# The second MLP product as seven quarter products (Strassen), with sums made by accumulating DMA

## The chip, the cores and the metric

The kernel runs on one core of a Trainium2 chip. The time is that of one execution on the device, in microseconds (us). The engines are TensorE (PE; its weight loads are shown as PEld), VectorE (DVE), ScalarE (ACT), GpSimd (POOL) and SyncE (SP), which only issues transfers.

## What is computed

One layer of a decoder trunk: four token mixers, gated and projected, then a two-layer MLP. The change touches the MLP alone. S = 512 tokens, D = 1024, hidden width 4096, all in 32-bit floats.

```python
hn = _rms(x, norm2_g[l])
hid = jnp.square(jax.nn.relu(jnp.einsum('bsd,df->bsf', hn, w_mlp1[l])))
x = x + jnp.einsum('bsf,fd->bsd', hid, w_mlp2[l])
```

## The kernel before

Every product with weights is made of three matmuls: each operand is split into a high part (`hi`, a cast by ScalarE, L74) and a low part (`lo`, the difference, a subtraction by VectorE, L75), and `mm3` (L78 to L81) adds high x high, high x low and low x high in PSUM. The first factor of a matmul stays in the array (128 x 128), the second streams through it, at most 512 columns.

Weights come as a stream of pieces of 512 KB (`piece`, L91). A piece has a `load` (a transfer on SyncE's queue into one of 4 buffers `raw`, L102) and a `make` (the split into `hi_m` and `lo_m`, 3 buffers each). `take` and `get` (L114 to L126) make two pieces ahead of the one in use and load two more. A buffer of `raw` comes free when its `lo` is made; one of `hi_m` when its matmuls are done. The order on each engine is settled by the framework's planner from its own estimate of readiness, within these dependencies.

The MLP begins at L946. The first product computes the hidden values transposed, 128 hidden rows by 512 tokens at a time (a piece `m1`: 8 x 3 = 24 matmuls into the PSUM tile `h`); `mlp1_done` (L958) applies relu on ScalarE, squares on VectorE and splits the result into `hdh` and `hdl`. This is done for half of the hidden rows (16 pieces), then the second product of this half follows (L986 to L1019): for each half `q` of the 1024 columns, 8 pieces `m2` of 256 hidden rows by 512 columns, each with 4 token tiles x 2 x 3 = 24 matmuls into four PSUM tiles `o`. After the last piece VectorE adds each `o` to `X1` (the residual, L1017), and in the second half SyncE stores the result (L1019). The last token tile's last columns are made as two halves of 256. Then the same for the second half of the hidden rows.

GpSimd issues some transfers in the attention part, among them copies from SBUF to SBUF (L402, L403); none in the MLP.

Of the kernel before, what the change touches and what calls it, by code (L numbers as in the profile page):

```python
# [8 lines left out]
F32 = mybir.dt.float32  # L9
# [7 lines left out]
P = 128  # L17
# [10 lines left out]
HPW = 268  # L28

# [8 lines left out]
def block_kernel(ctx: ExitStack, tc: tile.TileContext, x, w_in, w_branch, w_gate, w_out,  # L38
# [52 lines left out]
    def piece(name, srcs, nk, alloc=None):  # L91
# [22 lines left out]
    def get(i, ahead):  # L114
        while len(made) < min(i + 1 + ahead, len(pieces)):
            made.append(pieces[len(made)][1]())
        for j in range(len(made), min(len(made) + 2, len(pieces))):
            pieces[j][0]()
        return made[i]
# [40 lines left out]
    for q in range(2):  # L160
        for k in range(4):
            piece(f"wo{q}{k}", [w_out[k * 256 : (k + 1) * 256, q * 512 : (q + 1) * 512]], 2,
                  lambda tag, nm: wop[0].tile([P, 4 * HPW], F32R, tag=tag, name=f"{tag}_{nm}"))
    NH = NF // 2
    for fh in range(2):
        for f in range(fh * NH, (fh + 1) * NH):
            piece(f"m1_{f}", [w_mlp1[:, f * P : (f + 1) * P]], 8)
        for q in range(2):
            for f0 in range(fh * NH, (fh + 1) * NH, 2):
                piece(f"m2_{q}{f0}", [w_mlp2[f0 * P : f0 * P + 256, q * 512 : (q + 1) * 512]], 2)  # L170

# [795 lines left out]
    for fh in range(2):
        f = fh * NH
        if fh == 0:
            finish(*ttr[:2])  # L970
            w = take(3, 0)
            accs = [ps(f"h_{f + j}") for j in range(3)]
            for j in range(3):
                mlp1_part(accs[j], w[j], 0, 256)
            finish(*ttr)
            for j in range(3):
                mlp1_part(accs[j], w[j], 256, 512)
                mlp1_done(f + j, accs[j])
            f += 3
        while f < (fh + 1) * NH:  # L980
            w, = take()
            acc = ps(f"h_{f}")
            mlp1_part(acc, w, 0, 512)
            mlp1_done(f, acc)
            f += 1
        for q in range(2):  # L986
            if q == 0:
                acc = [ps(f"o_{fh}{q}{t}") for t in range(NT)]
            else:
                a2 = [ps2(f"o_{fh}{q}{t}") for t in range(2)]  # L990
                acc = [a2[t // 2][:, t % 2, :] for t in range(NT)]
            acc = [[(a, 0, 512)] for a in acc]
            if fh == 1 and q == 1:
                acc[-1] = [(ps(f"o_{fh}{q}h{i}")[:, :256], 256 * i, 256) for i in range(2)]

            def out_mm(fp, t, w, part):
                sl = slice(t * P, (t + 1) * P)
                a, c0, n = part
                for j in range(2):
                    h = hid[fh * NH + 2 * fp + j]  # L1000
                    mm3(a, (h[0][:, sl], h[1][:, sl]), (w[0][:, j, c0 : c0 + n], w[1][:, j, c0 : c0 + n]),
                        fp == 0 and j == 0, fp == NH // 2 - 1 and j == 1)


            for fp in range(NH // 2 - 2):
                w, = take()
                for t in range(NT):
                    for part in acc[t]:
                        out_mm(fp, t, w, part)
            w = take(2, 1)  # L1010
            for t in range(NT):
                for part in acc[t]:
                    for i in range(2):
                        out_mm(NH // 2 - 2 + i, t, w[i], part)
                    a, c0, n = part
                    cs = slice(q * 512 + c0, q * 512 + c0 + n)
                    nc.vector.tensor_tensor(out=X1[:, t, cs], in0=X1[:, t, cs], in1=a, op=ALU.add)  # L1017
                    if fh == 1:
                        nc.sync.dma_start(out[t * P : (t + 1) * P, cs], X1[:, t, cs])  # L1019
# [49 lines left out]
```

## Time and profile before

| | |
|---|---|
| median of 3 runs | 832.59 us (832.59 to 832.61) |
| profiled execution: from the first to the last instruction (span) | 831.0 us |
| profiled execution with what lies around the span (taken as the median) | 832.6 us |
| TensorE busy | 822.4 us, 4097 matmuls |
| VectorE busy | 426.7 us |
| ScalarE busy | 299.6 us |
| transfers | 81.34 MB, mean 98 GB/s |

Busy time is the time in which at least one instruction of the engine was under way. The record of a matmul is longer than its share of the engine, since the next one enters before it ends: the distance of two starts is what one costs.

### The profile page before, as it was taken

The page shows a single profiled execution, that of the slowest core. Times are in us where ns is not written, and L with a number is a line of the kernel's source. Part 1 is how long each engine was busy: PE and PEld are TensorE (multiplying, and loading weights), DVE is VectorE, ACT ScalarE, POOL GpSimd, SP SyncE. Part 2 cuts the span into 40 slices and gives each one's busy share as a digit, 9 for nine tenths or more (in the row PEclk, how much of TensorE's full clock was granted, in tenths as well). Part 3 has the DMA queues.
Part 4 walks back from the last instruction along what each step waited for, and adds up shares of the span by engine and source line. Part 5 has one row for each costly group of instructions (what it writes and reads, how often), then busy time and mean ns, then how long its engine had stood idle before and what let it go on. Part 6 is the DMA issues. An engine that isn't in the chain of part 4 may idle for free.

```text
span 831.0 us, 10391 instructions
## 1 busy us (share of the span) xinstructions
PE 822.4 (99%) x4097; PEld 674.7 (81%) x4097; DVE 426.7 (51%) x766; ACT 299.6 (36%) x507; POOL 86.1 (10%) x82
## 2 busy tenths in 40 slices
PE   7999999999999999999999999999999999999998
PEld 5989787777787888888888888888888888888887
DVE  5967764346999446734625754442232444442321
ACT  6636533444423325423515344341121334332110
POOL 6011011221443121220000000000000000000000
PEclk9999999999999999999999999999999999999999
DMA  9282222321222232333536032323233233223401
GB/s 307 81 196 60 87 66 79 87 77 52 63 65 89 77 91 87 97 93 91 198 142 175 3 102 80 98 103 101 77 102 102 81 96 102 101 77 102 152 26 51
DMA packets 108979, 81.34 MB, mean 98 GB/s; under 512 B 3873, under 2 KB 96321, under 8 KB 108930
## 3 DMA queue, kind: packets, MB, share of 16 engines
q1 hardware_dynamic: 107666, 76.61, 30.4%
q10 hardware_dynamic: 720, 2.62, 0.9%
q0 software_dynamic: 544, 1.45, 0.6%
q8 instruction: 32, 0.52, 0.3%
q14 instruction: 17, 0.14, 0.0%
HBM read 78.05 MB, written 2.10 MB: 96 GB/s over the span
## 4 chain that ended last, share of the span: by engine, by line
PE 97%; DMA 1%; SPq 1%; ACT 0%; DVE 0%; issue 0%
PE gt L79 7%; PE gt L81 7%; PE h L81 7%; PE h L79 7%; PE h L80 7%; PE gt L80 7%; PE o L79 7%; PE o L80 7%; PE o L81 7%; PE pj L79 2%; PE pj L81 2%; PE wo L80 2%; PE wo L79 2%; PE wo L81 2%; PE pj L80 2%; PE pv L548 2%
## 5 line engine op out<-in xcount | busy, mean ns | idle before, releaser
L75 DVE TENSOR_TENSOR lo_m<-raw_m,hi_m 128x1024 fp32r<-128x1024 f32 x64 | 78.4, 1225 | 176.8 <-ACT hi_m L74 176.8
L74 ACT CAST hi_m<-raw_m 128x1024 fp32r<-128x1024 f32 x64 | 67.1, 1049 | 195.9 <-PE o L81 107.1
L81 PE MATMUL h<-HH,lo_m 128*128 128x512 f32 (+1 forms) x280 | 104.9, 375 | 0.0
L79 PE MATMUL h<-HH,hi_m 128*128 128x512 f32 (+1 forms) x280 | 104.5, 376 | 0.2 <-ACT HH L74 0.2
L80 PE MATMUL h<-HL,hi_m 128*128 128x512 f32 (+1 forms) x280 | 104.5, 374 | 0.0
L79 PE MATMUL gt<-XH,hi_wg 128*128 128x512 f32 x256 | 101.8, 398 | 0.0
L81 PE MATMUL gt<-XH,lo_wg 128*128 128x512 f32 x256 | 101.2, 395 | 0.0
L80 PE MATMUL gt<-XL,hi_wg 128*128 128x512 f32 x256 | 100.7, 393 | 0.0
L79 PE MATMUL o<-hi_m,hdh 128*128 128x512 f32 x240 | 95.0, 396 | 0.0
L80 PE MATMUL o<-lo_m,hdh 128*128 128x512 f32 x240 | 94.9, 395 | 0.0
L81 PE MATMUL o<-hi_m,hdl 128*128 128x512 f32 x240 | 94.3, 394 | 0.0
L75 DVE TENSOR_TENSOR lo_wg<-raw_wg,hi_wg 128x1024 fp32r<-128x1024 f32 x32 | 39.1, 1222 | 61.9 <-ACT hi_wg L74 61.8
L74 ACT CAST hi_wg<-raw_wg 128x1024 fp32r<-128x1024 f32 x32 | 33.5, 1047 | 83.0 <-PE gt L80 57.9
L81 PEld LDWEIGHTS h<-HH,lo_m 128*128 128x128 f32 x280 | 52.7, 188 | 10.4
L80 PEld LDWEIGHTS h<-HL,hi_m 128*128 128x128 f32 x280 | 52.7, 188 | 10.2
L79 PEld LDWEIGHTS h<-HH,hi_m 128*128 128x128 f32 x280 | 52.3, 188 | 10.1 <-ACT HH L74 0.5
L526 POOL TENSOR_SCALAR p<-p,c 128x128 f32<-128x128 f32 (+3 forms) x32 | 42.8, 1347 | 153.8 <-DVE c L524 141.8
L81 PEld LDWEIGHTS gt<-XH,lo_wg 128*128 128x128 f32 x256 | 48.1, 188 | 11.8 <-issue 0.5
L80 PEld LDWEIGHTS gt<-XL,hi_wg 128*128 128x128 f32 x256 | 48.2, 188 | 10.7
L79 PEld LDWEIGHTS gt<-XH,hi_wg 128*128 128x128 f32 x256 | 48.1, 188 | 10.7 <-issue 0.3
L81 PEld LDWEIGHTS o<-hi_m,hdl 128*128 128x128 f32 x240 | 45.0, 188 | 11.0
L79 PEld LDWEIGHTS o<-hi_m,hdh 128*128 128x128 f32 x240 | 45.2, 188 | 10.6
(368 smaller groups left out, 1439.8 us busy)
## 6 DMA issues: line engine op xcount, KB each, us to landing
raw_m<-in_w_mlp_dram SPq DMA_DIRECT2D x64, 512.0 KB, 3.6
raw_wg<-in_w_gate_dram SPq DMA_DIRECT2D x32, 512.0 KB, 3.9
raw_wb<-in_w_branch_dram SPq DMA_DIRECT2D x16, 256.0 KB, 2.6
raw_wo<-in_w_out_dram SPq DMA_DIRECT2D x8, 512.0 KB, 4.2
x<-in_x_dram SPq DMA_DIRECT2D x4, 512.0 KB, 6.6
raw_kv<-in_w_in_dram SPq DMA_DIRECT2D x4, 512.0 KB, 4.7
w<-in_cmp_w_dram SPq DMA_DIRECT2D x4, 512.0 KB, 6.0
X<-in_x_dram ACTq DMA_DIRECT2D x4, 512.0 KB, 6.7
```

Source lines behind the costliest of these rows:

```text
L74: i = nc.scalar.copy(hi, src)
L75: (eng or nc.vector).tensor_tensor(out=lo, in0=src, in1=f32(hi), op=ALU.subtract)
L79: nc.tensor.matmul(dst, l[0], r[0], start=start, stop=False)
L80: nc.tensor.matmul(dst, l[0], r[1], start=False, stop=False)
L81: nc.tensor.matmul(dst, l[1], r[0], start=False, stop=stop)
L526: nc.gpsimd.tensor_scalar_mul(p_[:, b, :w], p_[:, b, :w], c2[:, b : b + 1])
L548: nc.tensor.matmul(dst[i], V[:, k, b, g * HD : (g + 1) * HD], pts[h - 1 + i][:, b, k * P : (k + 1) * P], start=False, stop=b == 1 and k == t)
```

## The change

The second product is hidden (512 x 4096) times weights (4096 x 1024). Both are cut in two by two quarters: hidden by token half `h` and half `k` of the hidden rows, weights by `k` and column half `n`. Seven products of quarters (256 x 2048 by 2048 x 512) replace the eight; each takes a quarter or a sum or difference of two from either side, and is added to or subtracted from one or two quarters of `X1`. `PROD` lists for each product the left quarters (h, k, sign), the right quarters (k, n, sign) and the targets (h, n, sign).

A quarter product goes in 8 pieces of 256 hidden rows: a weight piece of 256 x 512 and a left piece of 2 x 128 rows by 256 tokens, with 2 x 2 x 3 = 12 matmuls of 512 columns. The hidden values stay unsplit in one tile `HID`; the left piece is split when it is needed (tags `hc0`, `hc1`). Sums of weights (products 3, 4, 6, 7): the first quarter's piece is loaded by SyncE into one of 3 buffers `rsum`, and an accumulating DMA that GpSimd issues adds the second quarter's to it. A difference of weights (product 1): both are loaded and VectorE subtracts. Sums of left pieces (1, 6, 7): SyncE copies the first inside SBUF to one of 4 buffers `hc`, and an accumulating DMA adds the second. Differences of left pieces (2, 5): VectorE.

The order is: the first 16 pieces of the first product; then the other 16, each followed by a piece of product 3 (8 times) or 6 (8 times); then products 4, 2, 1, 5, 7. Products 1 to 6 gather in a PSUM tile of two banks and are added to `X1` by operations of 128 x 1024; finished quarters are stored after products 2, 1 and 5. Product 7 ends as the old kernel did, with a 512-wide tile and two of 256. The constants `RAWS` and `AHEAD` have the old values 4 and 2.

```diff
@@ weight stream @@
+    PROD = {
+        1: (((0, 0, 1), (1, 1, 1)), ((0, 0, 1), (1, 1, -1)), ((0, 0, 1), (1, 1, -1))),
+        2: (((1, 1, 1), (1, 0, -1)), ((0, 0, 1),), ((1, 0, -1), (1, 1, 1))),
+        3: (((0, 0, 1),), ((0, 1, 1), (1, 1, 1)), ((0, 1, 1), (1, 1, -1))),
+        4: (((1, 1, 1),), ((1, 0, 1), (0, 0, 1)), ((0, 0, -1), (1, 0, 1))),
+        5: (((0, 0, 1), (0, 1, -1)), ((1, 1, 1),), ((0, 0, 1), (0, 1, -1))),
+        6: (((1, 0, 1), (0, 0, 1)), ((0, 0, 1), (0, 1, 1)), ((1, 1, 1),)),
+        7: (((0, 1, 1), (1, 1, 1)), ((1, 0, 1), (1, 1, 1)), ((0, 0, 1),)),
+    }
+    hcp = []
+    def block_piece(name, prod, p, B, kh, A):
+        aq, bq, _ = PROD[prod]
+        st = {}
+        def load():
+            if st:
+                return
+            st["raw"] = raws = []
+            for i, (k, n, sign) in enumerate(bq):
+                r0 = (k * kh + 2 * p) * P
+                wv = B[r0 : r0 + 256, n * 512 : (n + 1) * 512].rearrange("(k p) c -> p k c", p=P)
+                if i and sign > 0:
+                    nc.gpsimd.dma_start(raws[0].rearrange("p (k c) -> p k c", k=2), wv, accum_op=ALU.add)
+                    continue
+                if len(bq) == 1 or i:
+                    raw = wp.tile([P, 4 * HPW], F32, tag="raw", name=f"raw_{name}{i}", bufs=RAWS)[:, :1024]
+                else:
+                    raw = hcp[0].tile([P, 1024], F32, tag="rsum", name=f"rsum_{name}", bufs=3)
+                nc.sync.dma_start(raw.rearrange("p (k c) -> p k c", k=2), wv)
+                raws.append(raw)
+            st["a"] = src = [A()[:, k * kh + 2 * p : k * kh + 2 * p + 2, h * 256 : (h + 1) * 256] for h, k, _ in aq]
+            if len(aq) == 2:
+                hs = hcp[0].tile([P, 2, 256], F32, tag="hc", name=f"hc_{name}", bufs=4)
+                if aq[1][2] > 0:
+                    nc.sync.dma_start(hs, src[0])
+                    nc.gpsimd.dma_start(hs, src[1], accum_op=ALU.add)
+                    del src[1]
+                src.append(hs)
+        def make():
+            load()
+            raw = st["raw"]
+            if len(raw) == 2:
+                nc.vector.tensor_tensor(out=raw[0], in0=raw[0], in1=raw[1], op=ALU.subtract)
+            w = [walloc(tag, name)[:, :1024] for tag in ("hi", "lo")]
+            split(raw[0], w[0], w[1])
+            src = st["a"]
+            if len(src) == 3:
+                nc.vector.tensor_tensor(out=src[2], in0=src[0], in1=src[1], op=ALU.subtract)
+            src = src[-1:]
+            a = [hcp[0].tile([P, 2, 256], F32R, tag=f"hc{i}", name=f"hc{i}_{name}", bufs=3) for i in range(2)]
+            split(src[0], a[0], a[1])
+            return [x.rearrange("p (k c) -> p k c", k=2) for x in w], a
+        pieces.append((load, make))
     NH = NF // 2
-    for fh in range(2):
-        for f in range(fh * NH, (fh + 1) * NH):
+    NP = NH // 2
+    M2_EARLY, M2_LATE = (3, 6), (4, 2, 1, 5, 7)
+    plan = [("f", f) for f in range(NH)]
+    for i in range(NH):
+        plan += [("f", NH + i), ("s", M2_EARLY[i // NP], i % NP)]
+    plan += [("s", prod, p) for prod in M2_LATE for p in range(NP)]
+    for it in plan:
+        if it[0] == "f":
+            f = it[1]
             piece(f"m1_{f}", [w_mlp1[:, f * P : (f + 1) * P]], 8)
...
@@ MLP @@
     right.close()
-    hp = right.enter_context(tc.tile_pool(name="hp", bufs=16, side="right", reuse_waits="tile"))
-    hid = {}
+    hp = right.enter_context(tc.tile_pool(name="hp", bufs=1, side="right", reuse_waits="tile"))
+    HID = hp.tile([P, NF, S], F32, name="HID")
+    hcp.append(hp)
+    def block_mm(dst, w, a, t, first, last, c0=0, n=512):
+        for j in range(2):
+            sl = slice(t * P, (t + 1) * P)
+            mm3(dst, (a[0][:, j, sl], a[1][:, j, sl]), (w[0][:, j, c0 : c0 + n], w[1][:, j, c0 : c0 + n]),
+                first and j == 0, last and j == 1)
+    def block_part(acc, p, np_):
+        w, a = take(1, 2)[0]
+        for t in range(2):
+            block_mm(acc[:, t, :], w, a, t, p == 0, p == np_ - 1)
+    def block_add(prod, acc):
+        for h, n, sign in PROD[prod][2]:
+            xv = X1[:, 2 * h : 2 * h + 2, n * 512 : (n + 1) * 512]
+            nc.vector.tensor_tensor(out=xv, in0=xv, in1=acc, op=op_of(sign))
 
...
     def mlp1_done(f, acc):
-        r = hp.tile([P, S], F32, tag="rl", name=f"rl_{f}", bufs=2)
+        r = HID[:, f, :]
...
-        hh = hp.tile([P, S], F32R, tag="hdh", name=f"hdh_{f}")
-        hl = hp.tile([P, S], F32R, tag="hdl", name=f"hdl_{f}")
-        split(r, hh, hl)
-        hid[f] = (hh, hl)
-
...
+    def finished(prod, acc):
+        block_add(prod, acc)
+        for h, n in {2: ((1, 0),), 1: ((1, 1),), 5: ((0, 1),)}.get(prod, ()):
+            for t in range(2 * h, 2 * h + 2):
+                cs = slice(n * 512, (n + 1) * 512)
+                nc.sync.dma_start(out[t * P : (t + 1) * P, cs], X1[:, t, cs])
+
+    acc = None
+    for it in plan[3:]:
+        if it[0] == "f":
+            f = it[1]
             w, = take()
+            h = ps(f"h_{f}")
+            mlp1_part(h, w, 0, 512)
+            mlp1_done(f, h)
+            continue
+        _, prod, p = it
+        if prod == M2_LATE[-1]:
+            break
+        if p == 0:
+            acc = ps2(f"o_{prod}")
+        block_part(acc, p, NP)
+        if p == NP - 1:
+            finished(prod, acc)
+
+    a0 = ps("o_l0")
+    a1 = [ps(f"o_l1{i}") for i in range(2)]
+    parts = [(0, a0, 0, 512), (1, a1[0][:, :256], 0, 256), (1, a1[1][:, :256], 256, 256)]
+    for p in range(NP - 2):
+        w, a = take(1, 2)[0]
+        for t, d, c0, n in parts:
+            block_mm(d, w, a, t, p == 0, False, c0, n)
+    wa = take(2, 1)
+    for t, d, c0, n in parts:
+        for i in range(2):
+            block_mm(d, wa[i][0], wa[i][1], t, False, i == 1, c0, n)
+        cs = slice(c0, c0 + n)
+        nc.vector.tensor_tensor(out=X1[:, t, cs], in0=X1[:, t, cs], in1=d, op=ALU.add)
+        nc.sync.dma_start(out[t * P : (t + 1) * P, cs], X1[:, t, cs])
```

## Rows read from the trace of the kernel before

**Rows 1.** The page, parts 1 and 2.
```profile
PE 822.4 (99%) x4097; PEld 674.7 (81%) x4097; DVE 426.7 (51%) x766; ACT 299.6 (36%) x507; POOL 86.1 (10%) x82
...
PEclk9999999999999999999999999999999999999999
DMA  9282222321222232333536032323233233223401
```

**Rows 2.** The page, part 4: the chain, by engine.
```profile
PE 97%; DMA 1%; SPq 1%; ACT 0%; DVE 0%; issue 0%
```

**Rows 3.** What TensorE waited for: line, releaser, us in total, times, longest.
```profile
PE g_n L297 <- DMA g1row<-in_norm_dram: 2.4, 1, 2.4
PE tr_n L315 <- DVE xs L305: 2.3, 1, 2.3
PE h L79 <- ACT HH L74: 0.2, 1, 0.2
...
```

**Rows 4.** Timeline of the second product's end: start, us, engine, line, operation.
```profile
823.31 0.40 PE L79 MATMUL o<-hi_m,hdh 128*128 128x512 f32 x1
...
825.87 0.40 PE L81 MATMUL o<-hi_m,hdl 128*128 128x512 f32 x1
```

**Rows 5.** Groups of instructions by line, 530 to 831 us: busy, mean ns, idle before.
```profile
L75 DVE TENSOR_TENSOR lo_m<-raw_m,hi_m 128x1024 fp32r<-128x1024 f32 x51 | 62.5, 1225 | 152.4 <-ACT hi_m L74 152.4
L74 ACT CAST hi_m<-raw_m 128x1024 fp32r<-128x1024 f32 x51 | 53.5, 1049 | 173.4 <-PE o L81 107.1 <-PE h L80 43.5 <-PE o_11h L81 22.8
...
L75 DVE TENSOR_TENSOR hdl<-rl,hdh 128x512 fp32r<-128x512 f32 x23 | 15.9, 692 | 15.8 <-ACT hdh L74 15.8
...
L74 ACT CAST hdh<-rl 128x512 fp32r<-128x512 f32 x22 | 13.7, 621 | 30.8 <-DVE rl L961 30.8
...
L1017 DVE TENSOR_TENSOR X<-X,o 128x512 f32<-128x512 f32 x15 | 10.3, 686 | 28.2 <-PE o L81 28.2
```

**Rows 6.** The weight buffers `raw_m`, 540 to 831 us: their transfers.
```profile
DMA to landing us min/median/max: 3.1/3.3/4.8
```

**Rows 7.** Stretches: busy us of each engine, granted clock, DMA share, GB/s.
```profile
10.00:20.00 10.00, 9.74 (x59) 8.87 (x58) 6.51 (x16) 7.00 (x11) 5.62 (x3) 1.00 1.11 357
12.00:16.00 4.00, 4.00 (x22) 4.00 (x22) 2.71 (x5) 3.11 (x4) 2.02 (x1) 1.00 1.06 384
412.00:416.00 4.00, 4.00 (x19) 3.27 (x18) 2.46 (x4) 1.47 (x3) 0.00 (x0) 1.00 0.97 346
734.00:775.00 41.00, 41.00 (x177) 33.04 (x177) 12.32 (x13) 9.08 (x10) 0.00 (x0) 1.00 0.27 90
657.00:734.00 77.00, 77.00 (x334) 62.55 (x333) 34.48 (x42) 30.33 (x42) 0.00 (x0) 1.00 0.34 102
5.00:10.00 5.00, 2.67 (x9) 1.51 (x8) 3.11 (x15) 3.53 (x8) 3.08 (x5) 1.00 1.04 331
...
50.00:56.00 6.00, 6.00 (x42) 5.33 (x42) 2.50 (x7) 2.12 (x3) 0.97 (x2) 1.00 1.08 257
```

**Rows 8.** What SyncE's queue waited for: us in total, times, longest.
```profile
SPq L102 <- DVE lo_m L75: 309.7, 60, 30.9
...
SPq L1019 <- DVE X L1017: 41.3, 8, 28.7
```

**Rows 9.** Timeline of ScalarE in the first product.
```profile
699.09 1.05 ACT L74 CAST hi_m<-raw_m 128x1024 fp32r<-128x1024 f32 x1 [2.01 <-PE h L80]
...
704.62 1.05 ACT L74 CAST hi_m<-raw_m 128x1024 fp32r<-128x1024 f32 x1 [1.98 <-PE h L80]
```

**Rows 10.** Timeline of VectorE, two operations back to back.
```profile
212.20 1.21 DVE L75 TENSOR_TENSOR lo_sC<-raw_sC,hi_sC 128x1024 fp32r<-128x1024 f32 x1
213.33 5.50 DVE L616 SCALAR_TENSOR_TENSOR cv<-Z,sm,cv 128x512 f32<-128x512 f32 x7
```

**Rows 11.** The tile `kc`: GpSimd's copies of 128 KB inside SBUF.
```profile
DMA to landing us min/median/max: 4.3/5.5/6.9
```

**Rows 12.** Timeline of GpSimd: the issue of such a copy.
```profile
49.91 0.54 POOL L402 DMA_DIRECT2D kc<-kc  x1 [30.65 <-ACT kc L400]
```

More of the change, by code (lines that the diff above doesn't have):

```diff
@@ L28 @@
 HPW = 268
+RAWS = 4
+AHEAD = 2
 C_GU, C_GV, C_Q, C_KC, C_KS, C_KW, C_NG = 0, 256, 512, 768, 1024, 1280, 1536
@@ L97, in load @@
                 return
-            raw = wp.tile([P, 4 * HPW], F32, tag="raw", name=f"raw_{name}", bufs=4)
+            raw = wp.tile([P, 4 * HPW], F32, tag="raw", name=f"raw_{name}", bufs=RAWS)
             rv = raw[:, : nk * n].rearrange("p (k c) -> p k c", k=nk)
@@ L116, in get @@
             made.append(pieces[len(made)][1]())
-        for j in range(len(made), min(len(made) + 2, len(pieces))):
+        for j in range(len(made), min(len(made) + AHEAD, len(pieces))):
             pieces[j][0]()
@@ L163, in block_kernel, with op_of @@
                   lambda tag, nm: wop[0].tile([P, 4 * HPW], F32R, tag=tag, name=f"{tag}_{nm}"))
-    NH = NF // 2
-    for fh in range(2):
-        for f in range(fh * NH, (fh + 1) * NH):
+    PROD = {
[7 rows of a table added]
+    }
+    hcp = []
+    def op_of(sign):
+        return ALU.add if sign > 0 else ALU.subtract
+    def block_piece(name, prod, p, B, kh, A):
[40 more added lines that the diff above has]
+        pieces.append((load, make))
@@ L167, in block_kernel @@
+    NH = NF // 2
+    NP = NH // 2
[7 more added lines that the diff above has]
+            f = it[1]
             piece(f"m1_{f}", [w_mlp1[:, f * P : (f + 1) * P]], 8)
-        for q in range(2):
-            for f0 in range(fh * NH, (fh + 1) * NH, 2):
-                piece(f"m2_{q}{f0}", [w_mlp2[f0 * P : f0 * P + 256, q * 512 : (q + 1) * 512]], 2)
+        else:
+            block_piece(f"m2_{it[1]}{it[2]}", it[1], it[2], w_mlp2, NH, lambda: HID)
@@ L958, in mlp1_done @@
     def mlp1_done(f, acc):
-        r = hp.tile([P, S], F32, tag="rl", name=f"rl_{f}", bufs=2)
+        r = HID[:, f, :]
         nc.scalar.activation(out=r, in_=acc, func=AF.Relu)
         nc.vector.tensor_tensor(out=r, in0=r, in1=r, op=ALU.mult)
-        hh = hp.tile([P, S], F32R, tag="hdh", name=f"hdh_{f}")
-        hl = hp.tile([P, S], F32R, tag="hdl", name=f"hdl_{f}")
-        split(r, hh, hl)
-        hid[f] = (hh, hl)
[L967 to L980, printed above, removed]
-            w, = take()
[L982 to L1019, printed above, removed]
@@ new lines, in block_kernel @@
+    finish(*ttr[:2])
+    w = take(3, 0)
+    accs = [ps(f"h_{j}") for j in range(3)]
+    for j in range(3):
+        mlp1_part(accs[j], w[j], 0, 256)
+    finish(*ttr)
+    for j in range(3):
+        mlp1_part(accs[j], w[j], 256, 512)
+        mlp1_done(j, accs[j])
+    def finished(prod, acc):
[4 more added lines that the diff above has]
+                nc.sync.dma_start(out[t * P : (t + 1) * P, cs], X1[:, t, cs])
```

## The prediction

> **What bounds the kernel now.** I read the page's busy shares first. TensorE is busy for 99% of the span, VectorE for 51%, ScalarE for 36%, GpSimd for 10% and idle in the second half, and the granted clock is full in all 40 slices [rows 1]. The DMA line of the same view says that the transfers are at two to three tenths through the MLP. The chain that ended last is 97% TensorE [rows 2], and the list of what TensorE waited for holds 5.1 us in all, of which 0.2 us lies in the MLP [rows 3]. So time can only be won here by giving TensorE fewer or shorter matmuls, and it is kept only if what prepares their operands stays ahead.
>
> How far ahead is it? In the second product twelve matmuls in a row start at 823.31 to 825.87, 11 steps of 0.2327 us [rows 4]; each is 512 columns wide, with its record of 0.39 us overlapping the next. A piece of weights (256 rows by 512 columns, 512 KB) feeds 24 of them, 5.58 us, and costs ScalarE 1.05 us and VectorE 1.23 us for its two halves [rows 5]. Its load lands 3.3 us after issue [rows 6]. In that stretch the DMA engines are busy 0.27 at 90 GB/s [rows 7]. SyncE's longest wait is for buffers to come free, not for data [rows 8]: loads run as far ahead as the buffers let them.
>
> **The change, part by part.**
>
> *Removed.* The second product has 4 x 32 x 2 x 3 = 768 matmuls of 512 columns (the last token tile's as halves). Seven products of 8 pieces with 12 matmuls each are 672. 96 x 0.2327 = **-22.3 us** of TensorE. The splitting of the 32 hidden tiles also goes (0.62 us of ScalarE, 0.69 us of VectorE each [rows 5]); TensorE hid both, so nothing is gained on the path.
>
> *Budget.* A piece of a quarter product now has 12 matmuls: 12 x 0.2327 = 2.79 us instead of 5.58. Everything that prepares a piece has half the time, and there are 56 pieces instead of 32. Forty of them (products 4, 2, 1, 5, 7) come one after another at the end: 40 x 2.79 = 111.7 us of TensorE. The other sixteen (3 and 6) alternate with first-product pieces of 5.53 us (the start-to-start time of the casts in [rows 9]), so 8.32 us a pair.
>
> *ScalarE:* 1.05 + 0.62 = 1.67 us a piece. Covered.
>
> *VectorE:* weights' low half 1.23, left low half 0.69, a difference of left operands 0.69, of weights 1.23. Products 3, 4, 6, 7: 1.92 us; 2 and 5: 2.61; 1: 3.15. Two additions to X1 per product, 512-wide 0.69 [rows 5], so 1.4 us each and about 0.3 us a piece, replace 16 such of before. Only product 1 is over 2.79: 3.45, or 8 x 0.66 = 5.3 us. Records overlap their successors: 212.20 to 213.33 is 1.13 us where the record says 1.21 [rows 10], so with 0.08 off each of its 3 operations it is 8 x 0.42 = 3.4 us. It lies beside the transfers of product 1, which are longer (below), so I add nothing.
>
> *Transfers.* Twelve quarters of weights are read instead of four: 12 x 8 = 96 pieces of 512 KB against 32. The best rates that the trace shows with the DMA engines full are 357 GB/s over 10 us, 384 over 4 us, and 346 at 0.97 (again 357 per full share) for the output projection's weights, which have the form of these pieces [rows 7]. At 357 a 512 KB load takes 1.47 us, and two take 2.94: already over 2.79.
>
> An accumulating DMA stands nowhere in this trace. From below: it moves its own bytes once, as a load does, 1.47 us. I exclude less, because it reads from the same place. From above: GpSimd's own copies inside SBUF landed 4.3 to 6.9 us after issue for 128 KB [rows 11], longer than a load of four times the bytes, and the stretch that holds them moves 257 GB/s at a full share, not 357 [rows 7]; I take three passes, 4.4 us. Between them I choose two passes, 2.94 us: the operation has to read what lies in the destination besides its source, so twice a load's bytes enter the DMA engines for the same bytes written.
>
> DMA time per piece is then, in products 4, 2, 1, 5, 7:
> 4: load 1.47 + accumulate 2.94 = 4.41. 2: 1.47. 1: two loads 2.94, left copy (256 KB) 0.73, left accumulate 1.47 = 5.14. 5: 1.47. 7: 4.41 + 0.73 + 1.47 = 6.61.
> Their sum is 19.10 us, times 8 = **152.8 us** against TensorE's 111.7. Products 2 and 5 leave 2 x 8 x 1.32 = 21 us of idle DMA time; the three buffers of sums can take 3 pieces of the next product (15 to 20 us), so nearly all of it is used, and the whole stretch lasts what its transfers last: **+41.1 us**. In product 3's pairs, with the first product's load at 102/0.34 = 300 GB/s [rows 7] (1.75 us), the transfers are 6.16 of 8.32 us; in product 6's 1.75 + 6.61 = 8.36. No stall there, and a head start for product 4 of up to three pieces, 13 us.
>
> Against that head start stands the time in which the transfers cannot be full: a sum's buffer is held from the load's issue (3.3) over GpSimd's issue (0.54 [rows 12]) and the accumulate (5.5 or more [rows 11]) to the end of the split (2.3), 11.6 us, and there are three, so 3.9 us a piece in products 4 and 7 even with the DMA idle. Between the load and the accumulate of a piece, GpSimd's queue waits for the load; behind it stand only later accumulates. Outputs of products 2, 1 and 5 go into SyncE's queue behind VectorE's additions (before: 8 such waits, 41 us, hidden [rows 8]); loads behind them wait until that product ends, and 2 MB of outputs move (6 us in before too). I set these off against the head start at zero net, with 13 us either way.
>
> *End and clock.* The last product ends as before: a 512-wide addition, two 256-wide ones and their stores; nothing. TensorE will pause within pieces; at 5 to 10 us it ran nine instructions, was busy 2.67 of 5 us and was granted full clock [rows 7], so I charge nothing for the clock.
>
> Sum: -22.3 + 41.1 = +18.8. The profiled execution's span is 831.0; the median is 832.6, and I keep the 1.6 around the span. **851.4 us.**
>
> One page weighs on the term that the trace does not hold. The Trainium skill (Collectives: The Full Stack, Part 3) states that a reduction in the DMA engines costs no time for the add, but reads both operands through the same ring and measured 1.93 times slower than a copy; no run shows it yet, and as an estimate from that page the time would be 849.
>
> **The rivals.**
>
> *Cheap accumulates, faster.* If an accumulate costs a load's pass, the late stretch is 8 x (2.94 + 1.47 + 4.41 + 1.47 + 4.41) = 117.6 us, 5.9 over TensorE; with the head start, 0 to 6 are left. 832.6 - 22.3 + 6 = 816. The point of decision: each further pass adds 35.2 us, and the gain is used up at 134.0 us of transfers, so at 1.47 passes. For it: the DMA engines are idle for 70% of the MLP. Against: two streams enter for one written. The engines' limit belongs here too: at the best rate, 384 GB/s, two passes give 142.1 us and 840.7; 407 GB/s (357 x 152.8 / 134.0) would have to be moved to break even, and of the 0.29 that I give this case 0.05 are for that. By the Trainium skill (DMA: Bandwidth & Descriptors, Bandwidth) 16 MB loads reached 425 GB/s; this trace's best is 384; as an estimate from that page the time would be 827.
>
> *Dear or chained accumulates, slower still.* Three passes: 152.8 + 35.2 = 188.0, so 832.6 - 22.3 + 76.3 = 886.6, and product 6's pairs rise to 10.6 us, +18 less buffers. For it: the copies of [rows 11]. The chain of three buffers belongs here when accumulates take 8 us to land: 14.1/3 = 4.7 us a piece, which then binds product 4 rather than the bytes.
>
> *Nothing to measure.* At 1.4 to 1.5 passes gain and loss cancel: 832.6.
>
> **How the numbers follow.** Forecast (two passes, DMA bounds the late products) 0.48, its own range 838 to 866; cheap 0.29; dear 0.18; cancelled 0.05. Range 815 to 886: it leaves out the best corner of the cheap case and half of the dear one. About 0.2% is what a measurement can tell from no change: faster 0.29, same 0.05, slower 0.66.
>
> **What would show it.** Right: TensorE waits in products 4, 1 and 7 and not in 2, 5, 3, with ScalarE's casts waiting for the accumulating DMA; DMA share near 1 in those three at some 240 to 360 GB/s. The step of two passes is read from the GpSimd queue's share against its bytes. Wrong: DMA share well below 1 while TensorE waits (then it is latency and buffers), or VectorE busy throughout product 1 with data landed (then VectorE bounds), or TensorE above 95% throughout, for the cheap case. A clock below 1.00 would break the last step.

## The result, and the profile after

| | before | after |
|---|---|---|
| median | 832.6 us | 859.41 us (858.50 to 859.82, 4 runs) |
| span of the profiled execution | 831.0 us | 858.1 us |
| ratio after to before | | 1.0319 [1.0304, 1.0333] |

The change costs 26.8 us; 18.8 were predicted. In the code after, the splits are L76 and L77 and the three matmuls L81 to L83 (each two lines further down than before); `rsum` is loaded at L203 and gets its accumulate at L197, the left sums are copied at L209 and accumulated at L210, VectorE's difference of weights is L218, and a finished product is added to `X1` at L1038.

The page after, parts 1, 2 and 4, to be held against [rows 1] and [rows 2]:

```profile
PE 818.8 (95%) x4001; PEld 662.4 (77%) x4001; DVE 491.2 (57%) x835; ACT 334.8 (39%) x555; POOL 153.7 (18%) x138
...
PEclk9999999999999999999999999999999998999979
DMA  9371322331222332333555755377899787899995
...
PE 80%; DMA 12%; DVE 3%; issue 2%; ACT 2%; SPq 0%; POOL 0%; ACTq 0%; POOLq 0%; DVEq 0%
DMA rsum_m<-in_w_mlp_dram 8%; PE gt L81 7%; PE gt L83 7%; PE gt L82 7%; PE h L81 7%; PE h L83 7%; PE h L82 7%; PE o L82 2%; PE o L83 2%; PE o L81 2%; PE pj L81 2%; PE pj L83 2%; PE wo L82 2%; PE wo L81 2%; PE wo L83 2%
```

TensorE has its 96 matmuls less, and the DMA line has gone from two or three tenths to eight or nine in the last quarter of the span. The largest single entry of the chain is no longer a matmul but the transfers into `rsum`.

What TensorE waited for, after (columns as in [rows 3]):

```profile
PE o_l L81 <- ACT hi_m L76: 11.2, 4, 8.6
PE o L82 <- DVE lo_m L77: 8.8, 15, 1.6
PE o L81 <- ACT hi_m L76: 5.3, 4, 2.1
...
```

All of these lie in the late products; `o_l` is product 7. Cut at VectorE's additions to `X1`, the stretches are: products 3 and 6 with the first product's pieces, then 4, 2, 1, 5, 7 (columns as in [rows 7]; a cut is good to about 2 us, since TensorE starts the next product before the addition):

```profile
560.20:626.80 66.60, 66.60 (x289) 53.91 (x288) 29.87 (x32) 24.64 (x33) 10.90 (x10) 1.00 0.80 186
626.80:693.40 66.60, 66.60 (x289) 53.90 (x288) 34.30 (x38) 24.78 (x32) 14.17 (x12) 1.00 0.90 210
693.40:731.40 38.00, 31.06 (x105) 22.35 (x104) 16.75 (x20) 14.12 (x18) 5.16 (x5) 0.87 0.82 183
731.40:758.10 26.70, 24.71 (x103) 18.83 (x101) 21.35 (x24) 11.00 (x14) 4.82 (x4) 1.00 0.93 272
758.10:789.80 31.70, 25.19 (x91) 16.56 (x92) 26.00 (x30) 13.75 (x18) 7.22 (x6) 1.00 1.08 326
789.80:814.30 24.50, 23.56 (x105) 18.57 (x104) 18.05 (x21) 12.16 (x17) 6.05 (x5) 1.00 1.02 246
814.30:854.20 39.90, 26.03 (x129) 21.49 (x129) 14.39 (x17) 9.10 (x11) 10.92 (x9) 0.83 0.89 195
```

Both early stretches have TensorE busy throughout. The five late products take 160.8 us where TensorE alone needs 111.7: 49.1 - 22.3 = 26.8, the whole result. The transfers' engine time in them is 0.82 x 38.0 + 0.93 x 26.7 + 1.08 x 31.7 + 1.02 x 24.5 + 0.89 x 39.9 = 150.7 us (what ran inside the stretch, stores and loads ahead among it). But the two products that lose most, 4 and 7, are the two in which the DMA engines are least full. What was waited for in product 4, and then in product 7:

```profile
DVE lo_m L77 <- ACT hi_m L76: 21.1, 6, 4.6
ACT hi_m L76 <- DMA rsum_m<-in_w_mlp_dram: 18.8, 5, 4.8
POOL rsum_m L197 <- DMA rsum_m<-in_w_mlp_dram: 14.1, 3, 6.7
```

```profile
ACT hi_m L76 <- DMA rsum_m<-in_w_mlp_dram: 22.3, 5, 10.4
```

One chain is seen here: load, GpSimd's accumulate, ScalarE's cast, VectorE's low half, matmul. Whether the bytes make it late or the three buffers do, these rows don't say.

### The profile page after: what moved, and what is told of

It reads as the page before. It is cut to its first block, busy times and chain, and to the rows that moved or that the text cites. A ratio compares the mean times of both kernels' runs of the same rounds, so it can differ in the third digit from the quotient of the medians.

```text
span 858.1 us, 10661 instructions
## 1 busy us (share of the span) xinstructions
PE 818.8 (95%) x4001; PEld 662.4 (77%) x4001; DVE 491.2 (57%) x835; ACT 334.8 (39%) x555; POOL 153.7 (18%) x138
## 4 chain that ended last, share of the span: by engine, by line
PE 80%; DMA 12%; DVE 3%; issue 2%; ACT 2%; SPq 0%; POOL 0%; ACTq 0%; POOLq 0%; DVEq 0%
DMA rsum_m<-in_w_mlp_dram 8%; PE gt L81 7%; PE gt L83 7%; PE gt L82 7%; PE h L81 7%; PE h L83 7%; PE h L82 7%; PE o L82 2%; PE o L83 2%; PE o L81 2%; PE pj L81 2%; PE pj L83 2%; PE wo L82 2%; PE wo L81 2%; PE wo L83 2%
## 5 line engine op out<-in xcount | busy, mean ns | idle before, releaser
L77 DVE TENSOR_TENSOR lo_m<-rsum_m,hi_m 128x1024 fp32r<-128x1024 f32 x40 | 49.0, 1225 | 111.1 <-ACT hi_m L76 111.1
L83 PE MATMUL h<-HH,lo_m 128*128 128x512 f32 (+1 forms) x280 | 105.0, 375 | 0.0
L81 PE MATMUL h<-HH,hi_m 128*128 128x512 f32 (+1 forms) x280 | 104.6, 376 | 0.2 <-ACT HH L76 0.2
L81 PE MATMUL gt<-XH,hi_wg 128*128 128x512 f32 x256 | 101.9, 398 | 0.0
L83 PE MATMUL gt<-XH,lo_wg 128*128 128x512 f32 x256 | 101.3, 396 | 0.0
L77 DVE TENSOR_TENSOR lo_m<-raw_m,hi_m 128x1024 fp32r<-128x1024 f32 x48 | 58.7, 1222 | 57.0 <-ACT hi_m L76 56.8
L197 POOL DMA_DIRECT2D rsum_m<-in_w_mlp_dram x32 | 39.0, 1218 | 290.7 <-DMA rsum_m<-in_w_mlp_dram 160.1
L76 ACT CAST hi_m<-rsum_m 128x1024 fp32r<-128x1024 f32 x40 | 41.9, 1047 | 124.4 <-PE h L82 67.9
L82 PE MATMUL o<-lo_m,hc_m 128*128 128x512 f32 x192 | 79.8, 416 | 8.8 <-DVE lo_m L77 8.8
L81 PE MATMUL o<-hi_m,hc_m 128*128 128x512 f32 x192 | 78.6, 409 | 7.2 <-ACT hi_m L76 5.3
L83 PE MATMUL o<-hi_m,hc_m 128*128 128x512 f32 x192 | 77.8, 406 | 0.4
L77 DVE TENSOR_TENSOR lo_wg<-raw_wg,hi_wg 128x1024 fp32r<-128x1024 f32 x32 | 39.1, 1222 | 62.0 <-ACT hi_wg L76 61.8
L76 ACT CAST hi_m<-raw_m 128x1024 fp32r<-128x1024 f32 x48 | 50.2, 1046 | 59.1 <-PE h L82 32.5
L599 POOL TENSOR_SCALAR p<-p,c 128x128 f32<-128x128 f32 (+3 forms) x32 | 42.7, 1346 | 157.3 <-DVE c L597 145.4
L76 ACT CAST hi_wg<-raw_wg 128x1024 fp32r<-128x1024 f32 x32 | 33.5, 1047 | 83.0 <-PE gt L82 58.0
L83 PEld LDWEIGHTS h<-HH,lo_m 128*128 128x128 f32 x280 | 52.7, 188 | 10.4
L81 PEld LDWEIGHTS h<-HH,hi_m 128*128 128x128 f32 x280 | 52.3, 188 | 10.2 <-ACT HH L76 0.5
L83 PEld LDWEIGHTS gt<-XH,lo_wg 128*128 128x128 f32 x256 | 48.1, 188 | 11.7 <-issue 0.5
```

The source lines that it names most:

```text
L76: i = nc.scalar.copy(hi, src)
L77: (eng or nc.vector).tensor_tensor(out=lo, in0=src, in1=f32(hi), op=ALU.subtract)
L81: nc.tensor.matmul(dst, l[0], r[0], start=start, stop=False)
L82: nc.tensor.matmul(dst, l[0], r[1], start=False, stop=False)
L83: nc.tensor.matmul(dst, l[1], r[0], start=False, stop=stop)
L197: nc.gpsimd.dma_start(raws[0].rearrange("p (k c) -> p k c", k=2), wv, accum_op=ALU.add)
```

## The experiments

Two theories. *Bytes*: the late stretch lasts as long as its transfers (the prediction). *Buffers*: a `rsum` buffer is held over two transfers that follow one another, and three of them can't feed TensorE, however full the DMA engines are. Each run stands beside runs of the kernel before on the same chip (medians 832.7 to 833.1). The five late products in all of the runs that the argument needs, in us, cut as above:

| kernel | median | 4 | 2 | 1 | 5 | 7 |
|---|---|---|---|---|---|---|
| TensorE alone | | 22.3 | 22.3 | 22.3 | 22.3 | 22.3 |
| after | 859.4 | 38.0 | 26.7 | 31.7 | 24.5 | 39.9 |
| e1_plain | 841.4 | 30.5 | 24.7 | 31.4 | 21.9 | 35.1 |
| e2_half | 838.3 | 28.8 | 25.5 | 30.5 | 21.1 | 32.7 |
| e3_rsum2 | 890.6 | 53.6 | 27.2 | 35.5 | 24.2 | 49.5 |
| e3_rsum4 | 856.2 | 28.3 | 27.3 | 46.4 | 21.6 | 33.0 |
| e4_dve | 828.4 | 26.2 | 24.1 | 29.5 | 23.7 | 25.0 |
| e9_ring | 845.0 | 22.7 | 26.0 | 33.8 | 22.7 | 40.2 |
| e11_ringleft | 825.7 | 22.4 | 25.1 | 29.0 | 28.7 | 21.0 |

**The price of an accumulate.** First the accumulates become plain transfers, then they cover only half.

```diff
-                    nc.gpsimd.dma_start(raws[0]..., wv, accum_op=ALU.add)
+                    nc.gpsimd.dma_start(raws[0]..., wv)
-                    nc.gpsimd.dma_start(hs, src[1], accum_op=ALU.add)
+                    nc.gpsimd.dma_start(hs, src[1])
```

> GpSimd's transfers stay, with their bytes, their order and their waits, but write instead of adding (so each sum is replaced by its second term: the adds are left out). If an accumulate is two passes of the DMA engines and the late products last as long as their transfers, these fall from 152.8 to 117.6 us and the time to 816 to 826 us; GpSimd's queue then takes about half the engine time per MB. If the chain of three buffers (load, wait, issue, landing, split) sets the pace instead, a plain transfer lands only little earlier and the time stays at 845 to 855 us.

```diff
+                    nc.gpsimd.dma_start(raws[0]...[:, 0:1], wv[:, 0:1], accum_op=ALU.add)
+                    nc.gpsimd.dma_start(hs[:, 0:1], src[1][:, 0:1], accum_op=ALU.add)
```

> Every accumulating DMA adds only the first half of its bytes (one of the two blocks of 128 rows; the other half of each sum is left out). By the theory of two passes per byte, half the bytes at two passes cost what all bytes cost at one: the late transfers fall to 117.5 us and the time to 816 to 826 us, the same as with plain transfers. If an accumulate has a large fixed price (issue and landing), little falls away: 845 to 855 us.

Measured 841.41 (1.0100 [1.0080, 1.0121]) and 838.28 (1.0063 [1.0039, 1.0087]), here and below with the ratio to before and its 95% interval. The DMA queues from 560 us to the end of the second product, after, then e1_plain, then e2_half; q0 is GpSimd's (packets, MB, share of the 16 engines):

```profile
q1 hardware_dynamic: 34497, 44.57, 45.6%
q0 software_dynamic: 13328, 20.45, 43.4%
```

```profile
q0 software_dynamic: 5776, 20.45, 22.9%
```

```profile
q0 software_dynamic: 7056, 10.23, 24.3%
```

Over 297, 280 and 274 us these are 128.9, 64.1 and 66.6 us of the engines: 6.30 us a MB for an accumulate, 3.13 for a plain transfer, ratio 2.01. Half of an accumulate costs what the whole of a plain one does, and the two kernels' times agree to 3 us. So two passes is right. But only 18 to 21 us came back, where 35.2 us of transfers were taken away: bytes alone are not the limit.

**More and fewer buffers for the sums.** Four `rsum` buffers fit only with one left buffer less.

```diff
-                    raw = hcp[0].tile([P, 1024], F32, tag="rsum", name=f"rsum_{name}", bufs=3)
+                    raw = hcp[0].tile([P, 1024], F32, tag="rsum", name=f"rsum_{name}", bufs=4)
-                hs = hcp[0].tile([P, 2, 256], F32, tag="hc", name=f"hc_{name}", bufs=4)
+                hs = hcp[0].tile([P, 2, 256], F32, tag="hc", name=f"hc_{name}", bufs=3)
```

> Four buffers for the sums of weights instead of three (and three instead of four for the left pieces, to make room; product 4 uses none of those). If the chain of buffers sets the pace of product 4 (4.75 us a piece with three, DMA share 0.82), four give 4.75 x 3/4 = 3.6 us or the transfers' own 3.9 us, whichever is more: product 4 falls from 38 to 29 to 33 us, the kernel to 845 to 853 us. If the bytes set it, product 4 stays at 38 us and the time at 857 to 860 us.

The other run has `bufs=2` for `rsum` and four left buffers.

> Two buffers for the sums of weights instead of three. If the chain sets the pace, a piece of products 4 and 7 takes 4.75 x 3/2 = 7.1 us less what an emptier DMA gives back (to 6): product 4 becomes 46 to 57 us, product 7 likewise, product 1 too (its first term uses these buffers), the kernel 880 to 910 us. If the bytes set it, the time stays within 5 us of 859.

Measured 856.16 (1.0294 [1.0264, 1.0325]) and 890.61 (1.0693 [1.0672, 1.0715]). Product 4 with four buffers, product 1 with them, and product 4 with two (columns as in [rows 7]):

```profile
693.40:721.70 28.30, 25.68 (x106) 19.49 (x106) 17.14 (x20) 14.02 (x18) 4.84 (x4) 1.00 0.92 227
...
749.00:795.40 46.40, 33.04 (x99) 22.55 (x99) 24.47 (x28) 13.19 (x18) 10.88 (x9) 0.78 1.01 272
```

```profile
694.00:747.60 53.60, 34.07 (x98) 24.59 (x97) 18.63 (x20) 13.87 (x17) 7.25 (x6) 0.75 0.69 149
```

Product 4, with the same bytes to gather, takes 53.6, 38.0 and 28.3 us with two, three and four buffers, and with two the DMA engines are the least busy (0.69). So buffers bind product 4. How long is one held? A buffer's next load is issued when its low half is made, so the time from a low half to the one that is made from the same buffer next, three pieces later in after, is a holding time. VectorE's low halves in after, e3_rsum2 and e3_rsum4, two from the same buffer each:

```profile
703.53 1.23 DVE L77 TENSOR_TENSOR lo_m<-rsum_m,hi_m 128x1024 fp32r<-128x1024 f32 x1 [3.21 <-ACT hi_m L76]
...
721.08 1.23 DVE L77 TENSOR_TENSOR lo_m<-rsum_m,hi_m 128x1024 fp32r<-128x1024 f32 x1 [4.37 <-ACT hi_m L76]
```

```profile
727.51 1.23 DVE L77 TENSOR_TENSOR lo_m<-rsum_m,hi_m 128x1024 fp32r<-128x1024 f32 x1 [3.26 <-ACT hi_m L76]
...
741.90 1.23 DVE L77 TENSOR_TENSOR lo_m<-rsum_m,hi_m 128x1024 fp32r<-128x1024 f32 x1 [6.37 <-ACT hi_m L76]
```

```profile
698.05 1.23 DVE L77 TENSOR_TENSOR lo_m<-rsum_m,hi_m 128x1024 fp32r<-128x1024 f32 x1 [0.26 <-ACT hi_m L76]
...
715.90 1.22 DVE L77 TENSOR_TENSOR lo_m<-rsum_m,hi_m 128x1024 fp32r<-128x1024 f32 x1 [1.10 <-ACT hi_m L76]
```

Over all pairs of product 4 the mean is 17.0 us with three buffers, 13.9 with two and 16.8 with four, so 5.7, 7.0 and 4.2 us a piece against TensorE's 2.79. The product lasts less than eight times that, because the first pieces are gathered before it begins. (Its time by eight, 4.75 us a piece in after, therefore understates the holding time; the expectations above took it for the pace.) The fourth buffer gained 9.7 us there and 6.9 in product 7, but the left buffer that it cost gave back 14.7 in product 1, whose TensorE now waits for the left sums:

```profile
PE o L81 <- ACT hc_m L76: 11.6, 5, 4.2
```

**Buffers from elsewhere.** Products 4 and 7 don't use the four `raw` buffers. Their odd pieces get them for their sums; all accumulates stay.

```diff
-                if len(bq) == 1 or i:
+                if len(bq) == 1 or i or (prod in (4, 7) and p % 2):
                     raw = wp.tile([P, 4 * HPW], F32, tag="raw", ...
```

> The changed kernel, but in products 4 and 7 every second sum of weights is gathered in one of the four load buffers that these products leave unused, so 7 buffers instead of 3 for the sums, and nothing else is given up. If the chain of buffers set the pace of these two products, they fall to what their transfers need: product 4 from 38 to 28 to 31 us (28 with four buffers in the run before), product 7 from 40 to 31 to 34, products 2, 1 and 5 as they were: 838 to 848 us. If it is the bytes, 855 to 860.

Measured 844.97 (1.0148 [1.0132, 1.0165]). Products 4 and 7, and what TensorE waited for in 7:

```profile
693.90:716.60 22.70, 22.70 (x100) 18.29 (x99) 17.19 (x20) 12.85 (x17) 1.20 (x1) 1.00 0.90 249
...
799.10:839.30 40.20, 26.38 (x142) 22.90 (x142) 16.61 (x19) 11.27 (x14) 9.66 (x8) 0.87 0.84 169
```

```profile
PE o_l L81 <- ACT hc_m L76: 14.1, 5, 5.6
```

With seven buffers product 4 runs without any wait, at unchanged bytes: better than the 28 to 31 us expected of it. The transfers that no longer wait for a buffer now run ahead, during product 6: GpSimd issues one accumulate within the stretch, where after has four. Product 7 gains nothing and misses its 31 to 34 us, since now its left sums are last: they are a copy and an accumulate one after the other too, with four buffers.

**The left sums by VectorE besides.** e9_ring, and

```diff
-                if aq[1][2] > 0:
-                    nc.sync.dma_start(hs, src[0])
-                    nc.gpsimd.dma_start(hs, src[1], accum_op=ALU.add)
-                    del src[1]
...
-                nc.vector.tensor_tensor(out=src[2], in0=src[0], in1=src[1], op=ALU.subtract)
+                nc.vector.tensor_tensor(out=src[2], in0=src[0], in1=src[1], op=op_of(aq[1][2]))
```

> The run with seven buffers for the sums of products 4 and 7 (845.0 us), and the three sums of left pieces by VectorE instead of copy and accumulating DMA. Weights' sums stay with the accumulating DMA. Transfers: product 1 falls from 5.14 to 2.94 us a piece, product 7 from 6.61 to 4.41; VectorE in product 1 rises to 3.5 us with its additions (29.5 us measured with all sums on VectorE). Expected: product 1 29 to 30 us instead of 32, products 2 and 5 at 23 to 24, product 7 28 to 31, 832 to 838 us. If the left sums by DMA cost nothing, 845; if the accumulating DMA for the weights is then still what separates this from all sums on VectorE, it stays above 828.4.

Measured **825.66** (824.94 to 826.10), 0.9916 [0.9899, 0.9933]: 7.0 us faster than the kernel before, 33.8 faster than after, and 6 us below the range expected. Products 4 to 7:

```profile
693.50:715.90 22.40, 22.40 (x98) 18.08 (x97) 16.89 (x20) 12.56 (x16) 1.20 (x1) 1.00 0.91 249
715.90:741.00 25.10, 24.70 (x106) 19.62 (x105) 24.01 (x29) 14.15 (x18) 0.00 (x0) 1.00 0.67 217
741.00:770.00 29.00, 24.31 (x96) 18.69 (x96) 27.45 (x33) 12.78 (x16) 1.20 (x1) 0.94 0.87 263
770.00:798.70 28.70, 25.57 (x112) 20.01 (x110) 21.14 (x27) 12.47 (x17) 7.25 (x6) 0.98 0.98 270
798.70:819.70 21.00, 20.45 (x123) 18.13 (x123) 15.56 (x19) 7.94 (x10) 1.20 (x1) 0.95 0.48 100
```

126.2 - 111.7 - 22.3 = -7.8, close to the measured -7.0. By product the expectation missed twice: 7 took 21.0 us instead of 28 to 31, 5 took 28.7 instead of 23 to 24. The three left sums by DMA had cost 845.0 - 825.7 = 19 us, with seven buffers for the weights' sums. This run also separates the theories best: at the prediction's own prices the late stretch of e11_ringleft carries 152.8 - 2 x 8 x 2.20 = 117.6 us of transfers (products 1 and 7 lose copy and accumulate, 0.73 + 1.47), exactly those of e1_plain, where all passes are single. Same transfer time, yet 126.2 us against 143.6: chains and buffers make the difference. (By the traces e11_ringleft's transfers took even more engine time from 560 us on, 0.805 x 263 = 212 us against 0.720 x 280 = 202.)

**All sums by VectorE.** No accumulating DMA at all; both terms are loaded by SyncE.

```diff
-                if i and sign > 0:
-                    nc.gpsimd.dma_start(raws[0]..., wv, accum_op=ALU.add)
-                    continue
...
-                nc.vector.tensor_tensor(out=raw[0], in0=raw[0], in1=raw[1], op=ALU.subtract)
+                nc.vector.tensor_tensor(out=raw[0], in0=raw[0], in1=raw[1], op=op_of(bq[1][2]))
```

(and the left sums as in e11_ringleft)

> All sums by VectorE: both terms are loaded by SyncE and added, no accumulating DMA at all. Transfers of the late products fall to 8 x (2.94 + 1.47 + 2.94 + 1.47 + 2.94) = 94 us, under TensorE's 111.7. VectorE then has per piece 3.2 (product 4), 3.8 (1) and 3.5 us (7) with its additions and 0.08 us off each operation: 8 x (0.4 + 1.0 + 0.7) = 17 us over TensorE. Transfers as the cause: about 828 us (825 to 835). If something else of the change costs the 27 us (the order of the stream, the splitting of the left pieces, the clock), it stays above 845.

Measured 828.44 (0.9945 [0.9925, 0.9965]), as expected; its interval and that of e11_ringleft overlap, so with enough buffers the weights' sums by accumulating DMA are not shown to be dearer than by VectorE. What TensorE waits for in its second half is VectorE:

```profile
PE o L82 <- DVE lo_m L77: 8.7, 5, 2.8
PE o_l L82 <- DVE lo_m L77: 4.4, 3, 2.8
```

**The weights' sums by GpSimd.** e4_dve with `nc.gpsimd.tensor_tensor` for the weights.

> Sums and differences of weights by GpSimd on the loaded pieces, those of left pieces by VectorE, no accumulating DMA. GpSimd's 128x1024 subtraction took 2.47 to 2.64 us in the kernel before, against 2.79 us a piece; VectorE falls to at most 2.6 us plus 0.3; the transfers to 94 us. By the theory that only the transfers bound the late products, TensorE's gain of 22 us comes through but for a few us: 812 to 820 us. If GpSimd and VectorE hinder each other at SBUF, GpSimd passes 2.79 us a piece in products 4, 1 and 7 and the time is 825 to 840.

Measured 847.13 (1.0161 [1.0144, 1.0178]): slower than either expectation; TensorE waits 26.4 us for VectorE's low halves. Groups from 560 us on, GpSimd's line and two of VectorE's (columns as in [rows 5]):

```profile
L211 POOL TENSOR_TENSOR rsum_m<-rsum_m,raw_m 128x1024 f32<-128x1024 f32 x37 | 101.9, 2763 | 177.2 <-DMA rsum_m<-in_w_mlp_dram 106.1 <-DMA raw_m<-in_w_mlp_dram 47.3 <-DVE hc_m L77 7.8
```

```profile
L77 DVE TENSOR_TENSOR lo_m<-rsum_m,hi_m 128x1024 fp32r<-128x1024 f32 x39 | 66.9, 1717 | 50.7 <-ACT hi_m L76 50.7
...
L1043 DVE TENSOR_TENSOR HID<-HID 128x512 f32<-128x512 f32 x17 | 22.7, 1334 | 0.0
```

VectorE's own subtractions, 1.23 us before [rows 5], take 1.72 on average while GpSimd adds, and the square of 128 x 512, 0.68 us after, takes 1.33. The Trainium skill (SBUF — State Buffer, Who interferes with whom) states that a VectorE instruction with two inputs in SBUF contends with a GpSimd instruction that reads SBUF; this trace agrees, and it prices it.

**A mix.** e4_dve, but in products 4 and 7 every odd piece's weights are summed by accumulating DMA (`if i and prod in (4, 7) and p % 2`).

> The kernel with all sums by VectorE (828.4 us; its late products took 128 us, VectorE busy 80 to 100% of them), but in products 4 and 7 every second piece of weights is summed by an accumulating DMA. VectorE loses 8 additions of 1.15 us, 9 us; the DMA engines gain 8 passes of 1.5 us and had 15 to 50% idle there. By the theory that the slowest supplier sets the time, 819 to 823 us. If a single accumulate delays the pieces behind it on ScalarE's or VectorE's queue (order by the planner, landing 5 to 8 us), nothing is won: 826 to 835.

Measured 847.19 (1.0174 [1.0157, 1.0191]): a miss, worse than e4_dve by 19 us. Product 4 and its largest wait:

```profile
693.90:732.10 38.20, 28.31 (x98) 20.93 (x97) 18.87 (x21) 12.56 (x17) 3.00 (x3) 0.84 0.68 179
```

```profile
ACT hi_m L76 <- DMA rsum_m<-in_w_mlp_dram: 21.3, 3, 8.5
```

Three waits of ScalarE, 7 us on average, hold it at after's 38 us, with the DMA engines at 0.68. All eight pieces still share the three `rsum` buffers, and ScalarE and VectorE take pieces in order, so an odd piece that is late holds the even one behind it: argued from these rows and the code, not tried apart. I had counted VectorE's time and the bytes, and not the buffers.

**The clock.** In products 4 and 7 of after the granted clock is below 1.00. Eight matmuls of which nothing is used follow each piece of product 4 and the first six of 7.

```diff
+        if prod == 4:
+            fill(8)
...
+        fill(8)
```

> After every piece of product 4 and of the first six of product 7, eight more matmuls of 512 columns into a PSUM tile that nobody reads (1.9 us of TensorE each time, 26 us in all, nothing left out). If the fallen clock (0.87 and 0.83 in these products) costs time, TensorE now stays busy, the clock stays at 1.00 and the time falls by up to 10 us in spite of the added work. If the pace is that of the operands, the fillers lie in the waits and the time changes by less than 5 us, clock up or not. Where TensorE were the bound after all, it would rise by 26 us.

Measured 858.33 (1.0313 [1.0293, 1.0333]). Product 4 of it:

```profile
694.40:730.50 36.10, 36.10 (x158) 29.21 (x157) 17.11 (x20) 13.59 (x18) 4.84 (x4) 1.00 0.78 186
```

The clock is back at 1.00 and the product lasts 36.1 us instead of 38.0. But TensorE is now busy for all of it, so the added matmuls may themselves hold it up, and 36.1 us is only the most that it takes at full clock. The least can be estimated from its last low half:

```profile
724.64 1.23 DVE L77 TENSOR_TENSOR lo_m<-rsum_m,hi_m 128x1024 fp32r<-128x1024 f32 x1 [7.51 <-ACT hi_m L76]
```

With some 2.5 us of matmuls behind it the product can't end before about 728.4, 34 us after its start. So the clock costs an estimated 2 to 4 us in product 4; the waits for operands cost the rest of the 15.7. In product 7 the clock stayed at 0.87, so its price there is open. The total is 1.1 us less, which is within the noise.

**Products moved into the early stretch.** e4_dve, with the pieces of product 1, then of 1 and 4, spread over products 3 and 6, to give the late ones more time.

```diff
-    M2_EARLY, M2_LATE = (3, 6), (4, 2, 1, 5, 7)
+    M2_EARLY, M2_MID, M2_LATE = (3, 6), (1,), (4, 2, 5, 7)
...
+        if i >= 2 and i % 2 == 0:
+            plan += [("s", prod, i // 2 - 1) for prod in M2_MID]
```

> The kernel with all sums by VectorE (828.4 us), and product 1, its slowest (29.5 us against TensorE's 22.3), no longer stands among the late products: one of its pieces follows every second pair of the earlier stretch, where VectorE had 30% idle. By the theory that the suppliers' time per piece bounds the late products and that the transfers are no longer it, product 1 costs 22.3 us there: 820 to 823 us. If the change of order costs TensorE waits of its own (two products open at once), 825 or more.

> As the run with product 1 moved into the earlier stretch, with product 4 beside it (26.2 us where it was, against 22.3; its sums gathered in two single PSUM tiles): 816 to 820 us if VectorE's 18.5 us per two pairs stay under TensorE's 22.2 there; above 823 if the earlier stretch is now bound itself.

Measured 829.36 (0.9960 [0.9945, 0.9975]), no better than e4_dve, and 840.39 (1.0097 [1.0075, 1.0118]), worse: two misses. The largest wait of TensorE in the first, and a stretch of the second:

```profile
PE o L81 <- DVE X L1039: 5.1, 1, 5.1
```

```profile
700.00:760.00 60.00, 50.65 (x204) 39.95 (x203) 43.47 (x51) 20.72 (x29) 0.00 (x0) 0.91 0.63 191
```

In the first a matmul waits for VectorE's addition of a product to `X1`, as more products are open at once. In the second TensorE is busy for 50.65 of 60 us in its longer early stretch; after's has no waits. That the idle time which I wanted to use was needed where it was is my reading; it was not tried apart.

## Why the prediction was right or wrong

**Removed matmuls, -22.3 us:** right. Early stretches without a wait, late ones with 111.7 us of matmuls, account for the result within half a us (26.8 against 27.1 between the two spans).

**An accumulate costs two passes:** right, 2.01. The Trainium skill (Collectives: The Full Stack, Part 3) gives 1.93 for a reduction against a copy, and the trace agrees. The cheap case and the case of three passes both fall.

**Transfers of 152.8 us in the late stretch:** about right, but the 150.7 us of above are not its measure, since they contain the stores and lack what was brought before 693.4. At the measured prices (6.30 us a MB for accumulates; 0.456 x 297 / 44.57 = 3.04 for the rest) the 12.6 MB of accumulates and 29.4 MB of loads and copies of these products are an estimated 169 us of engine time. Where the engines were full, the share read 1.08 (product 1) to 1.11 (the row that the prediction's 357 GB/s came from, [rows 7]), so this is 152 to 156 us. That products 2 and 5 would be used to load ahead also held: 0.93 x 26.7 = 24.8 and 1.02 x 24.5 = 25.0 us of engine time in them, where their own bytes are 11.8. It is why product 1 could take 31.7 us and not the 41.1 of its own transfers.

**"The whole stretch lasts what its transfers last":** this step failed, though its number nearly came out. It lasted 160.8 us. Product 4 is not bound so: its share is 0.82, the sign that the prediction had named for latency and buffers, and two, three, four and seven buffers give 53.6, 38.0, 28.3 and 22.7 us at the same bytes. e9_ring, with every byte of after, does the late stretch in 145.4 us, less than the 152.8 that were said to be its floor: transfers that find a buffer start before the stretch.

**Head start and chain "at zero net":** the mis-sized term. The chain was put at 11.6 us of holding time, 3.9 us a piece. In product 4 it was 17.0, 5.7 us a piece; the first pieces, gathered ahead, brought that down to 38.0/8 = 4.75. The right kind was in the text: a last sentence of the dear rival has 14.1/3 = 4.7 us a piece for accumulates that land in 8 us, binding product 4 rather than the bytes (that 4.7 meets 4.75 is luck, since it leaves out the head start). The accumulates of 512 KB landed in 6.9 us (5.5 or more was taken), the loads of `rsum` in 6.0 (3.3 was taken from [rows 6], at a DMA share of about 0.3), GpSimd's issue took 1.22 (0.54); with the split's 2.3 that is 16.4. Bytes and buffers work on one another here: a buffer was held for 13.9 us at a DMA share of 0.69 (e3_rsum2) and for 17.0 at 0.82. The same was left out for the left sums, which have two transfers in a row as well; e11_ringleft puts all of these at 19 us. How product 7 splits between its two chains isn't settled: it took 33.0 with four weight buffers and three left ones, 40.2 with seven and four, 21.0 with seven and VectorE for the left. From 790 to 850 us the left accumulates landed in 7.6 us in after (median), 6.1 with four weight buffers and 11.1 with seven: weights' accumulates that run ahead seem to delay the left ones, which no run tried apart.

**Products 2 and 5 without waits:** nearly. Product 2 lost 4.4 us. ScalarE's cast of product 1's first left sums waits 8.1 us for their transfer, and VectorE's first three differences 3.1 us for their loads, ahead of product 2's last pieces on the same queues:

```profile
ACT hc_m L76 <- DMA hc_m<-HID: 8.1, 2, 5.7
...
DVE rsum_m L218 <- DMA raw_m<-in_w_mlp_dram: 3.1, 3, 1.4
```

**VectorE beside the transfers in product 1, at nothing:** doubtful. VectorE is busy for 26.0 of 31.7 us and the DMA engines are full (1.08, 326 GB/s), so the transfers look like the bound. But e1_plain, with 0.73 us a piece less to transfer in product 1, took 31.4 us, and e11_ringleft and e4_dve, with 2.20 less, still took 29.0 and 29.5. ScalarE's casts of product 1 waited for VectorE's differences, in after and in e1_plain alike:

```profile
ACT hi_m L76 <- DVE rsum_m L218: 11.9, 5, 2.7
...
ACT hi_m L76 <- DVE rsum_m L218: 12.1, 5, 2.6
```

So the order difference, cast, low half probably sets its pace, at little more than the 27.6 us (8 x 3.45) that the prediction counted for VectorE; no run separates it from the loads.

**No charge for the clock:** wrong in kind, small in size where it was measured. It fell, and by e7_fill it costs an estimated 2 to 4 us in product 4; in product 7 (0.83) it was not priced.

So the size came out in part by luck, from errors that nearly cancel: bytes were taken as a floor where there was none, which is too long, and the chains too short, the weights' by 5.4 us of holding time (17.0 - 11.6), the left sums' not counted at all.

## What to carry to other kernels

A sum made by load and accumulate holds its buffer over two transfers one after the other: divide that time, taken from landings under load, by the number of buffers, and compare it with what the consumer takes for a piece, before any sum of bytes. Buffers that a stage leaves idle are the cheapest remedy (one line, 14 us here), and a sum of operands that already lie in SBUF belongs to an engine with time left, not to a transfer (19 us). Seven products in place of eight then gain 7 us of the 22 that TensorE saves.

## What the runs showed of the hardware

- An accumulating DMA took 6.30 us of the 16 engines' time per MB, a plain one 3.13; GpSimd's issue 1.22 us against 0.72.
- GpSimd's additions of 128 x 1024 took 2.76 us and stretched VectorE's subtractions from 1.23 to 1.72 us on average.
- The granted clock fell to 0.50 (1.2 GHz) in product 7, where TensorE had run no matmul from 822 to 826 us (after, columns as in [rows 7]):

```profile
822.00:826.00 4.00, 0.00 (x0) 0.00 (x0) 0.00 (x0) 0.00 (x0) 0.74 (x1) 0.82 1.08 254
826.00:830.00 4.00, 0.10 (x1) 0.11 (x1) 0.12 (x1) 1.20 (x2) 1.20 (x1) 0.50 1.15 253
830.00:834.00 4.00, 3.96 (x11) 3.10 (x12) 2.40 (x3) 0.98 (x2) 2.01 (x2) 0.50 1.14 220
```

With its matmuls back it still ran at that level: 11 records in 3.96 us, where 4 us at full clock held 18 (690 to 694 us).
